# The five-tap convolution of a state-space branch: accumulated in PSUM in three pieces per channel tile instead of in SBUF

## The chip, the cores and the metric

The kernel runs on one core of a Trainium2 chip. Five queues run beside each other on that core: the tensor engine (PE, with its weight loads shown apart as PEld), the vector engine (DVE), the scalar engine (ACT), GpSimd (POOL), and SyncE (SP), which here only issues DMAs. Each takes its instructions strictly in the order in which the program lists them, and waits where an instruction needs something that another engine has not delivered yet. The metric is the device time of one execution in microseconds (us).

## The reference

The program is a two-layer network over 1024 latent tokens and 256 context tokens, 1024 channels wide, in float32. The change lies in layer 0, whose mixer begins with one large input projection. Its results feed, among others, a state-space branch (through a convolution over 5 tokens) and a conformer branch (through a convolution over 31 tokens):

```python
def dwconv(t, w, b):
    pad = w.shape[0] // 2
    y = lax.conv_general_dilated(t, w[:, None, :].astype(t.dtype), window_strides=(1,), padding=[(pad, pad)],
                                 dimension_numbers=('NWC', 'WIO', 'NWC'), feature_group_count=t.shape[-1])
    return y + b

def ssd_branch(z, xbc, dt_raw, h0_f, h0_b, conv_w, conv_b, ...):
    xbc = jax.nn.silu(dwconv(xbc, conv_w, conv_b))        # 5 taps, 1536 channels
...
def conformer_conv(glu_in, w, b, ln_g, ln_b):
    val, gt = jnp.split(glu_in, 2, axis=-1)
    h = dwconv(val * jax.nn.sigmoid(gt), w, b)            # 31 taps, 1024 channels
    return jax.nn.silu(layer_norm(h, ln_g, ln_b))
```

Context (256 tokens) and latents (1024 tokens) are convolved apart, each with its own zero padding.

## The kernel before

The stage in question is `inproj0`. Channels lie on the 128 partitions, tokens along the free dimension. One channel tile is a projection of 128 channels for all 1280 tokens, in three slices of 512, 512 and 256 tokens, one PSUM bank each. Three banks (m0, m1, m2) rotate, so PE can be three slices ahead of the engine that copies a slice out. Each slice is 24 matmuls at L170 (8 parts of the contraction, three products each, for the split of float32 numbers into a high and a low part: `hhi`, `hlo`, `wh`, `wl`). The weights of a tile come by DMA; ACT rounds the high part (`wh`, L157) and DVE subtracts for the low part (`wl`, L158).

The tiles come in this order: GLU tiles 0 to 6 of the conformer branch (a gate and a value projection each), then the twelve tiles of the state-space branch, then GLU tile 7. These twelve are called tiles 1 to 12 here. The first matmul of tile 1 starts at 272.72 us of the profiled execution, and the value projection of GLU tile 7 starts at 510.48 us; this stretch is called the five-tap stage. It holds thirteen projections: tiles 1 to 12 and the gate of GLU tile 7.

For each of the twelve tiles, `xbc` does this:

- POOL zeroes the edges of a buffer `pad` (L1231; two buffers, so tile n waits until the taps of tile n-2 have read theirs).
- ACT copies the three slices out of PSUM to `pad` (L1235).
- ACT multiplies by the first tap into `acc5` in SBUF (L1242), over all 1282 positions.
- DVE does taps 2 to 5, one instruction each over all 1282 positions (L1244): `acc = pad * w + acc`, with `pad` and `acc` both in SBUF.
- ACT applies the silu in two parts (L1245, L1246), and SP stores the two parts (L1247, L1248).

Beside it run the 31-tap convolutions of the GLU tiles, as work to fill in. For GLU tiles 1, 3 and 6 ACT makes the products (L1215, two buffers `prod`) and POOL adds them up (L1216, `accq`, all in SBUF), 30 adds per GLU tile, with a start by ACT (L1212) and a copy back by ACT (L1217, L1218). For the others DVE does 30 steps (L1224): `acc = u * w + acc`, with `u` in SBUF and `acc` in PSUM. In the five-tap stage POOL finishes GLU tile 3 and does GLU tile 6; DVE finishes GLU tile 4 and does GLU tile 5.

The order on every engine is set at build time by a scheduler that estimates durations; the five-tap convolution has high priority and the 31-tap steps a very low one (-3000 and -5000), so they fill what the scheduler believes to be gaps.

## Time and profile before

| what | us |
|---|---|
| median of 3 runs (2262.7 to 2266.95) | 2266.37 |
| the profiled execution, first to last instruction | 2267.6 |
| the five-tap stage in it, 272.72 to 510.48 | 237.8 |
| PE busy in the whole execution | 2148.1 |
| PE idle, waiting for the copy of a slice to `pad` | 35.2 |
| DVE busy in the five-tap stage | 229.3 |

The page of the profile gives busy time by engine, the work that ended last, and the costliest groups of instructions with the idle time before them and what ended it. The trace answers with the waits by pairs of engines, with the instructions of an engine in order of time (start, duration, engine, line, operation, output, inputs, count; in brackets the idle time before, if any), and with the busy time of each engine and the granted clock of PE in any stretch. An instruction's duration overlaps the next one's by up to a tenth of a microsecond, so what a step costs is best read from the distance of two starts.

### The profile page before, as it was taken

What the parts mean: (1) busy time and instruction counts of PE and PEld (TensorE: products, weight loads), DVE (VectorE), ACT (ScalarE), POOL (GpSimd) and SP (SyncE); (2) the same over time, 40 slices, a digit from 0 to 9 for tenths busy, and PEclk for the clock granted to TensorE, in tenths of its full rate; (3) what the DMA queues carried; (4) which work ended last, traced back from release to release, by engine and by line L of the source; (5) the groups of instructions that cost most, each with busy time, mean ns of one, the idle gap of its engine ahead of it and who ended that gap; (6) DMA issues with size and microseconds to landing.
All of it is one profiled execution on the core that took longest, in us unless ns stands there. A gap on an engine that the chain in (4) does not pass through costs nothing.

```text
span 2267.6 us, 28582 instructions
## 1 busy us (share of the span) xinstructions
PE 2148.1 (95%) x10748; PEld 1647.3 (73%) x10748; DVE 1470.1 (65%) x1912; ACT 1005.1 (44%) x1553; POOL 1015.7 (45%) x652
## 2 busy tenths in 40 slices
PE   7998998889999999999999999999999999899997
PEld 6877876769997766656789788888666666666676
DVE  6799999988743377677775133223665566566677
ACT  4355565543552233333333233325556666545510
POOL 0088998870223355444330128433344444424453
PEclk9999999989999999899999999999999999899998
DMA  7121111115535765555434224323112111523363
GB/s 271 57 67 57 42 51 64 63 59 170 180 113 191 249 194 176 169 192 180 140 115 134 75 77 170 128 84 98 51 45 60 31 45 53 161 83 116 111 187 128
DMA packets 160145, 262.79 MB, mean 116 GB/s; under 512 B 19028, under 2 KB 98768, under 8 KB 159752
## 3 DMA queue, kind: packets, MB, share of 16 engines
q1 hardware_dynamic: 158584, 257.45, 34.9%
q0 software_dynamic: 1280, 3.26, 0.5%
q8 instruction: 84, 1.38, 0.2%
q14 instruction: 53, 0.43, 0.1%
q10 hardware_dynamic: 144, 0.26, 0.0%
HBM read 186.55 MB, written 74.32 MB: 115 GB/s over the span
## 4 chain that ended last, share of the span: by engine, by line
PE 58%; DVE 7%; DMA 5%; ACT 3%; issue 2%; POOL 2%; SPq 0%; POOLq 0%; DVEq 0%; ACTq 0%
PE m L170 28%; PE m L1009 12%; PE po L746 4%; PE st L728 2%; PE st L729 1%; PE ms L691 1%; DMA mr<-in_modw_dram 1%; PE m L840 1%; PE po L1542 1%; DVE ml L158 1%; PE ms L686 1%; ACT rb L433 1%; POOL ks L828 1%; PE m L691 1%; PE yd L1563 1%
## 5 line engine op out<-in xcount | busy, mean ns | idle before, releaser
L170 PE MATMUL m<-hhi,wh 128*128 128x512 f32 (+1 forms) x840 | 306.9, 369 | 36.8 <-ACT pad L1235 35.2
L1216 POOL TENSOR_TENSOR accq<-accq,prod 128x1295 f32<-128x1295 f32 x90 | 319.0, 3545 | 43.7 <-ACT prod L1215 30.3
L170 PE MATMUL m<-hlo,wh 128*128 128x512 f32 (+1 forms) x840 | 308.2, 367 | 0.0
L170 PE MATMUL m<-hhi,wl 128*128 128x512 f32 (+1 forms) x840 | 306.1, 365 | 1.0 <-DVE wl L158 1.0
L1224 DVE SCALAR_TENSOR_TENSOR acc<-u,vwh,acc 128x1295 f32<-128x1295 f32 x150 | 234.8, 1565 | 6.1 <-issue 2.2
L739 POOL TENSOR_TENSOR pl<-pt,ph 128x512 fp32r<-128x512 f32 x96 | 129.0, 1344 | 236.7 <-ACT ph L738 227.7
L170 PE MATMUL m<-h1hi,wh 128*128 128x512 f32 (+1 forms) x544 | 218.3, 401 | 2.0 <-ACT rb L433 1.4
L170 PE MATMUL m<-h1lo,wh 128*128 128x512 f32 (+1 forms) x544 | 217.0, 399 | 0.0
L170 PE MATMUL m<-h1hi,wl 128*128 128x512 f32 (+1 forms) x544 | 216.3, 398 | 0.0
L170 PEld LDWEIGHTS m<-hhi,wh 128*128 128x128 f32 x840 | 161.7, 194 | 64.4 <-ACT pad L1235 38.3
L1009 PE MATMUL m<-woh,yh 128*128 128x512 f32 x448 | 187.0, 421 | 0.6 <-ACT yh L157 0.2
L1009 PE MATMUL m<-wol,yh 128*128 128x512 f32 x448 | 185.3, 414 | 1.0 <-DVE wol L158 0.5
L1009 PE MATMUL m<-woh,ylo 128*128 128x512 f32 x448 | 185.0, 413 | 0.5 <-DVE ylo L158 0.5
L170 PEld LDWEIGHTS m<-hhi,wl 128*128 128x128 f32 x840 | 162.6, 194 | 27.9 <-issue 3.4
L170 PEld LDWEIGHTS m<-hlo,wh 128*128 128x128 f32 x840 | 163.0, 194 | 24.6 <-issue 2.4
L1215 ACT ACTIVATE prod<-u,vwh 128x1295 f32<-128x1295 f32 x90 | 123.4, 1378 | 82.0 <-POOL accq L1216 81.9
L738 ACT CAST ph<-pt 128x512 fp32r<-128x512 f32 x152 | 93.1, 619 | 115.3 <-PE po L746 107.9
L158 POOL TENSOR_TENSOR wl<-wr,wh 128x1024 fp32r<-128x1024 f32 x33 | 80.6, 2443 | 122.7 <-ACT wh L157 99.0
L1244 DVE SCALAR_TENSOR_TENSOR acc<-pad,vecs,acc 128x1282 f32<-128x1282 f32 x48 | 131.8, 2748 | 3.2 <-issue 1.8
L170 PEld LDWEIGHTS m<-h1hi,wh 128*128 128x128 f32 x544 | 103.2, 190 | 28.7 <-issue 2.6
L746 PE MATMUL po<-ph,vs 128*66 128x512 f32 x304 | 122.9, 404 | 0.8 <-ACT ph L738 0.8
L731 ACT ACTIVATE pt<-st 128x512 f32<-128x512 f32 x152 | 90.7, 597 | 74.2 <-PE st L729 54.5
(360 smaller groups left out, 4890.2 us busy)
## 6 DMA issues: line engine op xcount, KB each, us to landing
wr<-in_wch_dram SPq DMA_DIRECT2D x69, 512.0 KB
mr<-in_modw_dram SPq DMA_DIRECT2D x64, 256.0 KB
mr<-in_modw_dram SPq DMA_DIRECT2D x16, 512.0 KB
wor<-in_wout_dram SPq DMA_DIRECT2D x16, 512.0 KB
xcT<-xbc_d SPq DMA_DIRECT2D x20, 320.0 KB
xt_d<-xtok SPq DMA_DIRECT2D x20, 320.0 KB
xtok<-xt_d SPq DMA_DIRECT2D x10, 640.0 KB
xt<-xt_d SPq DMA_DIRECT2D x10, 640.0 KB
```

Source lines behind the costliest of these rows:

```text
L158: (nc.gpsimd if pool_lo else nc.vector).tensor_tensor(lo, src, hi.bitcast(F32), op=ALU.subtract)
L170: nc.tensor.matmul(out, x(k), y(k), start=(c == 0), stop=(c == tot - 1))
L691: nc.tensor.matmul(ps[:, :nw], mv1[0:64, b, h], ks1[0:64, C + w0 * P:C + w0 * P + nw], start=True, stop=True)
L731: nc.scalar.activation(p.rearrange("p h t -> p (h t)"), ps, AF.Exp, scale=0.125)
L738: nc.scalar.copy(ph, p)
L739: (nc.gpsimd if x in (0, 1, 3) else nc.vector).tensor_tensor(pl, p, ph.bitcast(F32), op=ALU.subtract)
L746: nc.tensor.matmul(po[:66], vs[:, kb, v], p[y], start=first and i == 0, stop=last and i == 2)
L1009: nc.tensor.matmul(ps[f], y[u][:, k], w[k][v][:, 512 * f:512 * f + 512], start=i + j == 0, stop=i + j == 9)
L1215: nc.scalar.activation(pr, u[:, k:k + N], AF.Copy, scale=vwh[:, i, k:k + 1])
L1216: nc.gpsimd.tensor_tensor(acc, acc, pr, op=ALU.add)
L1224: nc.vector.scalar_tensor_tensor(acc[:, :N], u[:, k:k + N], vwh[:, i, k:k + 1], acc[:, :N], op0=ALU.mult, op1=ALU.add)
L1244: nc.vector.scalar_tensor_tensor(acc, pad[:, k:k + N], w(k), acc, op0=ALU.mult, op1=ALU.add)
```

## The change

`acc` becomes a PSUM tile. The convolution of a channel tile is cut in three pieces of 256, 512 and 512 tokens; each piece takes one of the two buffers of the PSUM bank name `ms`, gets its first tap from ACT, four taps from DVE, and a silu from ACT which writes to an SBUF buffer `out`. One store takes the place of two. The two positions between context and latents that were computed and dropped are no longer computed. The rest of the diff only removes comments.

```diff
             self.proj_ch(wp, W[i], hhi, hlo, ev)
             with tc.high_priority():
-                N = 1282
-                acc = p5.tile([P, 1282], F32, name="acc5", tag="acc5")
                 w = lambda k: self.V("cw", 5 * i + k)
-                nc.scalar.activation(acc, pad[:, 0:N], AF.Copy, scale=w(0))
-                for k in range(1, 5):
-                    nc.vector.scalar_tensor_tensor(acc, pad[:, k:k + N], w(k), acc, op0=ALU.mult, op1=ALU.add)
-                nc.scalar.activation(acc[:, :C], acc[:, :C], AF.Silu, bias=self.V("cb", i))
-                nc.scalar.activation(acc[:, 258:], acc[:, 258:], AF.Silu, bias=self.V("cb", i))
-                nc.sync.dma_start(xbc_d[i, :, :C], acc[:, :C])
-                nc.sync.dma_start(xbc_d[i, :, C:], acc[:, 258:])
+                out = p5.tile([P, T], F32, name="acc5", tag="acc5")
+                for a, n in ((0, 256), (256, 512), (768, 512)):
+                    o = a if a < C else a + 2
+                    acc = self.bank("ms")[:, :n]
+                    nc.scalar.activation(acc, pad[:, o:o + n], AF.Copy, scale=w(0))
+                    for k in range(1, 5):
+                        nc.vector.scalar_tensor_tensor(acc, pad[:, o + k:o + k + n], w(k), acc, op0=ALU.mult, op1=ALU.add)
+                    nc.scalar.activation(out[:, a:a + n], acc, AF.Silu, bias=self.V("cb", i))
+                nc.sync.dma_start(xbc_d[i], out)
```

In the changed kernel the first tap is L1244, the other taps L1246 and the silu L1247. The scheduler orders the stage anew. On POOL, from the adds of GLU tiles 1 and 3 on (the first 54 or 57 adds; each group of three MEMSETs prepares the `pad` of one tile, from tile 3 on):

```order
-L1216 TENSOR_TENSOR accq<-accq,prod 128x1295 x54
+L1216 TENSOR_TENSOR accq<-accq,prod 128x1295 x57
+L1231 MEMSET pad 128x2 x3
+L1216 TENSOR_TENSOR accq<-accq,prod 128x1295 x4
+L1231 MEMSET pad 128x2 x3
+L1216 TENSOR_TENSOR accq<-accq,prod 128x1295 x6
+L1231 MEMSET pad 128x2 x3
+L1216 TENSOR_TENSOR accq<-accq,prod 128x1295 x7
+L1231 MEMSET pad 128x2 x3
+L1216 TENSOR_TENSOR accq<-accq,prod 128x1295 x6
```

The adds now stand some six to a tile; before, three to five stood between two groups of MEMSETs in the same part.

On DVE, the taps of tile 1 (`ms` is the piece in PSUM; `acc` of L1224 is a 31-tap step):

```order
+L1246 SCALAR_TENSOR_TENSOR ms<-pad,vecs,ms 128x256
 L1224 SCALAR_TENSOR_TENSOR acc<-u_792,vwh,acc 128x1295
-L1244 SCALAR_TENSOR_TENSOR acc_2781<-pad,vecs,acc_2781 128x1282
+L1246 SCALAR_TENSOR_TENSOR ms<-pad,vecs,ms 128x512
+L1246 SCALAR_TENSOR_TENSOR ms<-pad,vecs,ms 128x256
 L1224 SCALAR_TENSOR_TENSOR acc<-u_792,vwh,acc 128x1295
-L1244 SCALAR_TENSOR_TENSOR acc_2781<-pad,vecs,acc_2781 128x1282
+L1246 SCALAR_TENSOR_TENSOR ms<-pad,vecs,ms 128x512
```

One tap of 1282 between two 31-tap steps has become one or two shorter taps. In tiles 3 to 5, seven or eight 31-tap steps stand in a tile instead of about four, and from tile 7 on none is left.

On ACT, one tile in the middle of the stage before, from the first copy of tile 6 to the first copy of tile 7 (`m_...` are slices in PSUM):

```order
L1235 COPY pad<-m_3193 128x512
L1215 ACTIVATE prod<-u_794,vwh 128x1295
L1235 COPY pad<-m_3219 128x512
L1215 ACTIVATE prod<-u_794,vwh 128x1295
L157 CAST wh<-wr 128x1024
L1235 COPY pad<-m_3245 128x256
L1242 ACTIVATE acc_3271<-pad,vecs 128x1282
L1215 ACTIVATE prod<-u_794,vwh 128x1295
L1245 ACTIVATE acc_3173<-acc_3173,vecs 128x256
L1246 ACTIVATE acc_3173<-acc_3173,vecs 128x1024
L1235 COPY pad<-m_3291 128x512
```

and in the changed kernel, between the last copy of tile 6 and the first copy of tile 7:

```order
L1215 ACTIVATE prod<-u_794,vwh 128x1295
L1247 ACTIVATE acc_3225<-ms,vecs 128x256
L1215 ACTIVATE prod<-u_794,vwh 128x1295
L1244 ACTIVATE ms<-pad,vecs 128x512
L1215 ACTIVATE prod<-u_794,vwh 128x1295 x2
L1247 ACTIVATE acc_3225<-ms,vecs 128x512
L1244 ACTIVATE ms<-pad,vecs 128x256
L1215 ACTIVATE prod<-u_794,vwh 128x1295
L157 CAST wh<-wr 128x1024
L1215 ACTIVATE prod<-u_794,vwh 128x1295
L1247 ACTIVATE acc_3225<-ms,vecs 128x512
L1235 COPY pad<-m_3369 128x512
```

Three products a tile have become six, and all of them stand ahead of the next tile's first copy. The last product of GLU tile 6 in the changed kernel stands between the first and the second copy of tile 9 (`m_3591`, `m_3617`):

```order
L1215 ACTIVATE prod<-u_794,vwh 128x1295
L1247 ACTIVATE acc_3447<-ms,vecs 128x512
L1215 ACTIVATE prod<-u_794,vwh 128x1295
L1244 ACTIVATE ms<-pad,vecs 128x256
L1247 ACTIVATE acc_3447<-ms,vecs 128x512
L1235 COPY pad<-m_3591 128x512
L1215 ACTIVATE prod<-u_794,vwh 128x1295
L1244 ACTIVATE ms<-pad,vecs 128x512
L1247 ACTIVATE acc_3558<-ms,vecs 128x256
L1235 COPY pad<-m_3617 128x512
```

Before, it stood between the first and the second copy of tile 11. PE's order of work in the stage is the same in both. Behind the stage only a few transposes of the output projection's stage (L1058, around 1150 us) change places with matmuls, and 12 stores fewer are issued by SP.

## Rows read from the trace of the kernel before

**Rows 1.** Costliest groups of the page: busy, mean ns | idle before, releaser.

```profile
L170 PE MATMUL m<-hhi,wh 128*128 128x512 f32 (+1 forms) x840 | 306.9, 369 | 36.8 <-ACT pad L1235 35.2
L1216 POOL TENSOR_TENSOR accq<-accq,prod 128x1295 f32<-128x1295 f32 x90 | 319.0, 3545 | 43.7 <-ACT prod L1215 30.3
...
L1244 DVE SCALAR_TENSOR_TENSOR acc<-pad,vecs,acc 128x1282 f32<-128x1282 f32 x48 | 131.8, 2748 | 3.2 <-issue 1.8
```

**Rows 2.** Busy time by stretch: length, PE, PEld, DVE, ACT, POOL, PE clock, DMA.

```profile
272.70:510.50 237.80, 201.07 (x963) 168.90 (x961) 229.25 (x113) 132.14 (x144) 205.30 (x84) 0.92 0.18 59
```

**Rows 3.** PE in order of time: starts of tile 1, tile 2, last projection.

```profile
272.72 0.40 PE L170 MATMUL m<-hhi,wh 128*128 128x512 f32 x1
...
286.50 0.40 PE L170 MATMUL m<-hhi,wh 128*128 128x512 f32 x1
...
510.48 0.50 PE L170 MATMUL m<-hhi,wh 128*128 128x512 f32 x1 [0.74 <-ACT th L1192]
```

**Rows 4.** Waits in the five-tap stage: total us, times, longest.

```profile
ACT acc L1245 <- DVE acc L1244: 52.4, 10, 14.0
ACT prod L1215 <- POOL accq L1216: 49.0, 32, 2.8
...
PE m L170 <- ACT pad L1235: 35.2, 10, 9.1
```

**Rows 5.** DVE in order of time: 31-tap steps, evacuations and five-tap steps.

```profile
269.86 0.68 DVE L1199 SCALAR_TENSOR_TENSOR u<-th,m 128x512 f32<-128x512 f32 x1
270.46 4.78 DVE L1224 SCALAR_TENSOR_TENSOR acc<-u,vwh,acc 128x1295 f32<-128x1295 f32 x3
...
277.22 0.41 DVE L1199 SCALAR_TENSOR_TENSOR u<-th,m 128x256 f32<-128x256 f32 x1
277.56 1.56 DVE L1224 SCALAR_TENSOR_TENSOR acc<-u,vwh,acc 128x1295 f32<-128x1295 f32 x1
279.03 1.21 DVE L158 TENSOR_TENSOR wl<-wr,wh 128x1024 fp32r<-128x1024 f32 x1
...
343.75 1.55 DVE L1244 SCALAR_TENSOR_TENSOR acc<-pad,vecs,acc 128x1282 f32<-128x1282 f32 x1
...
354.12 2.81 DVE L1244 SCALAR_TENSOR_TENSOR acc<-pad,vecs,acc 128x1282 f32<-128x1282 f32 x1
356.85 1.56 DVE L1224 SCALAR_TENSOR_TENSOR acc<-u,vwh,acc 128x1295 f32<-128x1295 f32 x1
```

**Rows 6.** All 150 instructions of L1224: duration in ns, least, median, most.

```profile
L1224 DVE SCALAR_TENSOR_TENSOR acc<-u,vwh,acc x150: 1551/1567/1574, 97.5 to 574.5; 128x1295 f32<-128x1295 f32 x150
```

**Rows 7.** ACT in order of time: products, and the change from GLU tile 3 to 6.

```profile
279.02 1.39 ACT L1215 ACTIVATE prod<-u,vwh 128x1295 f32<-128x1295 f32 x1 [0.77 <-POOL accq L1216]
...
283.14 1.38 ACT L1215 ACTIVATE prod<-u,vwh 128x1295 f32<-128x1295 f32 x1 [2.26 <-POOL accq L1216]
286.23 1.39 ACT L1215 ACTIVATE prod<-u,vwh 128x1295 f32<-128x1295 f32 x1 [1.71 <-POOL accq L1216]
...
337.80 0.41 ACT L1217 COPY u<-accq 128x256 f32<-128x256 f32 x1 [1.15 <-POOL accq L1216]
...
340.81 1.47 ACT L1212 ACTIVATE accq<-u,vecs,vwh 128x1295 f32<-128x1295 f32 x1
```

**Rows 8.** POOL in order of time: adds of GLU tiles 3 and 6.

```profile
229.89 83.25 POOL L1216 TENSOR_TENSOR accq<-accq,prod 128x1295 f32<-128x1295 f32 x24 [7.76 <-ACT accq L1212]
...
345.48 26.52 POOL L1216 TENSOR_TENSOR accq<-accq,prod 128x1295 f32<-128x1295 f32 x7
...
409.41 2.94 POOL L1216 TENSOR_TENSOR accq<-accq,prod 128x1295 f32<-128x1295 f32 x1
...
462.72 12.15 POOL L1216 TENSOR_TENSOR accq<-accq,prod 128x1295 f32<-128x1295 f32 x3
```

**Rows 9.** Busy time by stretch around one wait of PE (columns as in rows 2).

```profile
460.00:470.00 10.00, 4.84 (x17) 3.77 (x16) 10.00 (x6) 5.33 (x7) 8.51 (x6) 0.68 0.40 118
```

**Rows 10.** DVE in order of time: last weight split ahead of the next stage.

```profile
519.73 0.89 DVE L158 TENSOR_TENSOR zl<-wr,zh 128x704 fp32r<-128x704 f32 x1 [0.84 <-ACT zh L157]
```

## The prediction, made before the changed kernel ran

> **What bounds the kernel now.** I read the page's costliest groups first, then the busy time by stretch, then the waits of the one stretch that stood out, then three engines in order of time in it. PE is busy nearly throughout, and its largest idle time by far is 36.8 us, of which 35.2 us end with ACT's copy of a slice to `pad` [rows 1]. All of it lies in the five-tap stage [rows 4]. There PE needs 286.50 - 272.72 = 13.78 us for a projection when nothing holds it [rows 3]. Thirteen projections are 179.1 us, and the stage takes 510.48 - 272.72 = 237.8 us, so 58.6 us are lost: 237.80 - 201.07 = 36.7 us with PE idle, and 21.9 us with PE busy at less than full clock, 0.92 on the mean [rows 2]. [...]
>
> The copies come late because ACT takes its instructions in order, and stands 52.4 us before silus that wait for DVE's last tap and 49.0 us before products that wait for POOL's adds [rows 4]. So DVE and POOL pace the stage, and they pace each other. A five-tap step beside POOL takes 2.81 us; the same step at 343.75, while POOL waited for its next convolution (337.8 to 345.48), took 1.55 us [rows 5, 7, 8]. POOL's add of the same size takes 286.23 - 283.14 = 3.09 us while DVE does only 31-tap steps [rows 7]. With five-tap and 31-tap steps in turn, one pair takes (356.85 - 354.12) + (279.03 - 277.56) = 4.20 us [rows 5], and the adds keep that pace (12.15 us for three) [rows 8]. The 31-tap step, with its accumulator in PSUM, takes 1551 to 1574 ns in all 150 cases, beside POOL or not [rows 6]. So what makes DVE and POOL stop for each other here is the instruction with two operands in SBUF, and the change turns 48 of these into the harmless form. The subtraction for `wl` stays as it is.
>
> **DVE's taps.** Removed: four steps of 2.73 us a tile, 10.9 us. Added: eight steps of 512 and four of 256. The nearest rows are the evacuations of GLU, one operand in PSUM, at 270.46 - 269.86 = 0.60 and 277.56 - 277.22 = 0.34 us from start to start [rows 5], which gives 8 x 0.60 + 4 x 0.34 = 6.2 us a tile; by their full durations, 0.68 and 0.41, it is 7.1 us. I take 6.5, since in most places a 31-tap step stands between two taps that depend on each other. DVE gets some 4.4 us a tile, 53 us in all, out of 229 busy [rows 2]. That is not the gain, because the scheduler puts 31-tap steps into it.
>
> [...]
>
> **POOL's adds, which lead.** After the change I price an add at 3.09 us, and at 4.12 (283.14 - 279.02) where a `wl` falls in [rows 7]. GLU tile 3 starts at 229.89 as before [rows 8]: 30 x 3.09 + 4 x 1.03 = 96.8, end at 326.7. Then ACT copies back and starts GLU tile 6: from 337.80 to 340.81 + 1.47 it took 4.5 us before [rows 7]; with some 2 us for ACT being at a silu, the adds of GLU tile 6 begin at about 333, not 345.48.
>
> **ACT's order.** In the middle of the stage six or seven products stand between the copies of one tile and of the next, and each waits for POOL, so a tile now takes 6 x 3.09 + 1.03 = 19.6 to 22.7 us there. That is above PE's 13.78, so PE will still wait 4 to 8 us in each of tiles 4 to 8. DVE must keep up: seven or eight steps of 1.47, 6.5 for taps and some 2 us for `wl` (1.21 at 279.03 [rows 5], more where it must wait for one) are 18.8 to 20.3 us, just under POOL's. The copies of tile 8 stand behind the 26th add's product, which waits for the 24th add: 333 + 24 x 3.09 + 5 x 1.03 = 412.3, then the product and two or three short steps of ACT, 415.5. From there four products are left, while PE has five projections to do: tile 9 starts when the first copy of tile 8 frees its bank.
>
> **The tail.** With no 31-tap steps left, a tile in the tail needs 6.5 to 8 us of DVE (more where taps of one piece follow each other directly) and 1.2 to 2 for `wl`, below 13.78. POOL's sums for the conformer stand ahead of the MEMSETs of tiles 11 and 12; at 4 us each, after adds that end near 431, they are done before 460, when tile 12 wants its buffer. So PE runs through: 415.5 + 5 x 13.78 = 484.4. The clock was low for some ten microseconds around a wait [rows 9], which I price at 10 x (1 - 0.68) = 3.2 at most and 2.5 here: 487. The value projection of GLU tile 7 starts 23.5 us earlier than at 510.48.
>
> **What follows it.** PE is then the leader for the next 70 us, so the gain stays only if nothing is late. The 31-tap steps of GLU tile 7 start behind PE's own value projection and move with it. The last weight split of the next stage ended at 520.6, 3 us before that projection did [rows 10]; it hangs on stores of tile 12 that now come about 480, more ahead of PE than before, so this cover grows. One store instead of two frees SP's queue. The few transposes that change places 650 us later cost PE the same. I count all of these at nothing; without that cover, each microsecond by which the split is late would be one of the gain.
>
> **Sum.** 23.5 us off the median of 2266.4 is 2242.9. The profiled execution spans 2267.6, 0.05% over the median, so its durations carry over. The bounds of the likeliest case: with adds at 2.94 us, as the one at 409.41 [rows 8], and no loss of clock, 54 x 0.15 + 2.5 = 10.6 us more gain, 2232; with DVE's `wl` and POOL's adds holding each other for another 1.5 us in five tiles and 3 us more of low clock, 10.5 less, 2253.
>
> **The rivals.**
>
> *Taps in PSUM hold POOL all the same, slower.* The instruction still reads `pad` in SBUF. If an add stayed at 4.20 us, the 35 adds from the first tap of tile 1 to the copies of tile 8 would cost 35 x 1.11 = 39 us more: 415.5 becomes 454, and the stage ends at 526, 15 us late: 2282. It decides from an add of 3.09 + 23.5 / 35 = 3.76 us on. For it: the changed order puts six adds ahead of each copy instead of three. Against it: 31-tap steps read SBUF once too, and the adds beside them take 3.09. 4 in 100.
>
> *Twelve short taps cost DVE more than four long ones.* If POOL were not what stretches a step to 2.81 us, and four long taps cost 1.55 each where it matters, twelve taps at full duration, 7.1 us a tile, would replace four at 1.55, 6.2, and a stage led by DVE would grow by 12 x 0.9 = 11 us: 2277. It decides once short taps take more than the long ones that they replace. Against it stands the step of 1.55 in POOL's pause beside 2.81 with POOL at work. 3 in 100. [...]
>
> *A new lock-step, no change.* If DVE falls behind in tiles 4 to 8, ACT waits at silus, products come late, and POOL waits too. Each of the five tiles would have to take 23.5 / 5 = 4.7 us more than counted, about 25 us. DVE's 20.3 is that near to POOL's pace only if each `wl` loses 4 us. 2266, 7 in 100.
>
> *PE leads from the start.* Then the stage is 179.1 us and the time 2266.4 - 58.6 = 2208. Against it: ACT's order has the products ahead of the copies. 3 in 100; something between this and the forecast is another 3.
>
> **How the numbers follow.** The forecast, 2232 to 2253, has 80 in 100. I widen the range to 2228 to 2260 for half-way cases on both sides. A gain or loss of under 0.2%, 4.5 us, can't be told from no change in this kernel: faster 0.87 (forecast, larger gains, half of what lies between), same 0.06, slower 0.07.
>
> **What would show it.** Right: 512-wide taps of 0.6 to 0.7 us with little spread; adds near 3.09 us in the stage; the last add of GLU tile 6 near 431 instead of 474.9; PE's waits for copies still there in tiles 4 to 8 (20 to 35 us in all) and next to none behind tile 8; the value projection of GLU tile 7 at about 487. Wrong: adds at 4 us, waits of POOL or DVE for ACT in the middle tiles, waits of PE in tiles 9 to 12, or a gain in the stage that is given back before 600 us.

## The result, and the profile after

The changed kernel took 2236.8 us (median of four runs, 2231.1 to 2244.1), the kernel before 2264.5 us beside it; the ratio is 0.988, 95% interval 0.985 to 0.992. The profiled execution after spans 2236.7 us, against 2267.6 before. In a later session the same changed kernel took 2242.8 us, the kernel before 2264.8 beside it, ratio 0.990 (0.987 to 0.993); the two intervals overlap.

Two groups of the page of after answer to [rows 1]; the columns are those of [rows 1].

```profile
L170 PE MATMUL m<-hhi,wh 128*128 128x512 f32 (+1 forms) x840 | 303.7, 365 | 21.0 <-ACT pad L1235 20.2
L1216 POOL TENSOR_TENSOR accq<-accq,prod 128x1295 f32<-128x1295 f32 x90 | 286.8, 3187 | 49.8 <-ACT prod L1215 32.0
```

PE's idle time at this group fell from 36.8 to 21.0 us, and the mean add of POOL from 3545 to 3187 ns. Next the two starts on PE that answer to [rows 3] (tile 1, value projection of GLU tile 7), and the busy time by stretch of what lies between (columns as in [rows 2]).

```profile
274.12 0.40 PE L170 MATMUL m<-hhi,wh 128*128 128x512 f32 x1
...
483.04 0.40 PE L170 MATMUL m<-hhi,wh 128*128 128x512 f32 x1
```

```profile
274.10:483.10 209.00, 188.80 (x939) 160.78 (x938) 186.30 (x209) 138.97 (x179) 169.26 (x84) 0.95 0.19 68
```

For the kernel before, the end of the stage has to be put right first. At 510.48 us, which [rows 3] takes for the start of the value projection of GLU tile 7, that projection's second slice starts, behind a wait for ACT's `th`. Its first slice starts at 503.68, 13 x 72 matmuls behind the start of tile 1 as in the changed kernel:

```profile
503.68 0.63 PE L170 MATMUL m<-hhi,wh 128*128 128x512 f32 x1
```

```profile
272.70:503.70 231.00, 195.02 (x939) 164.28 (x938) 224.72 (x111) 130.04 (x140) 205.30 (x84) 0.92 0.19 60
```

So the stage before is 503.68 - 272.72 = 231.0 us, not 237.8, and 51.8 us of it are lost, not 58.6. After, it takes 483.04 - 274.12 = 208.9 us: 22.0 us less. DVE is busy for 186 us instead of 225, POOL for 169 instead of 205, and PE's clock is 0.95 on the mean instead of 0.92. Ahead of the stage little moved (274.1 us against 272.7). Behind it, 2236.7 - 483.0 = 1753.7 us stand against 2267.6 - 503.7 = 1763.9, but the second execution of the changed kernel has 1760.5. Of the difference to the first, 5.8 us lie in one stretch of attention work over 1100 us behind the stage: 600 matmuls took 164.4 us before, at a granted clock of 0.96 in the mean (0.50 from 1750 to 1760 us), and 158.6 after, at 1.00. With three `pad` tiles the changed kernel took 164.5 us for them too, so this comes and goes and is no gain of the change.

The waits of the stage (total, times, longest) answer to [rows 4]:

```profile
ACT prod L1215 <- POOL accq L1216: 38.7, 30, 2.6
...
PE m L170 <- ACT pad L1235: 20.2, 6, 5.6
ACT acc L1247 <- DVE ms L1246: 11.1, 9, 2.4
```

ACT's wait for DVE's last tap fell from 44.2 us (52.4 in [rows 4], which run to 510.5) to 11.1; its wait for POOL's adds fell less, from 49.0 to 38.7. What is left of PE's waiting has a plain picture on ACT. These are the copies of tiles 6 and 7 of after, in order of time, with some of the products between them:

```profile
377.59 1.34 ACT L1235 COPY pad<-m 128x512 f32<-128x512 f32 x3
...
382.68 1.38 ACT L1215 ACTIVATE prod<-u,vwh 128x1295 f32<-128x1295 f32 x1 [1.33 <-POOL accq L1216]
...
385.77 1.39 ACT L1215 ACTIVATE prod<-u,vwh 128x1295 f32<-128x1295 f32 x1 [1.13 <-POOL accq L1216]
388.85 1.38 ACT L1215 ACTIVATE prod<-u,vwh 128x1295 f32<-128x1295 f32 x1 [1.69 <-POOL accq L1216]
...
396.85 1.34 ACT L1235 COPY pad<-m 128x512 f32<-128x512 f32 x3
```

From tile 4 to tile 7 all three copies of a tile are issued in one go, behind products that wait for POOL, and 396.85 - 377.59 = 19.3 us lie between two such groups, where PE needs 13.78 for a tile. In the stretch from tile 4 to tile 8 POOL is busy for 75.4 of 77.0 us, and DVE for 73.6 (columns as in [rows 2]):

```profile
337.00:414.00 77.00, 62.55 (x288) 52.43 (x288) 73.64 (x78) 55.53 (x68) 75.43 (x37) 0.89 0.18 62
```

### The profile page after: what moved, and what is told of

Same layout as the page of the kernel before. It is cut to its first block, busy times and chain, and to the rows that moved or that the text cites. A ratio compares the mean times of both kernels' runs of the same rounds, so it can differ in the third digit from the quotient of the medians.

```text
span 2236.7 us, 28691 instructions
## 1 busy us (share of the span) xinstructions
PE 2127.9 (95%) x10748; PEld 1636.1 (73%) x10748; DVE 1429.8 (64%) x2008; ACT 1013.3 (45%) x1589; POOL 983.6 (44%) x652
## 4 chain that ended last, share of the span: by engine, by line
PE 48%; DVE 5%; DMA 2%; ACT 2%; POOL 2%; issue 1%; SPq 0%; POOLq 0%; DVEq 0%; ACTq 0%
PE m L170 20%; PE m L1009 11%; PE po L746 4%; PE st L728 2%; PE st L729 1%; PE ms L691 1%; PE m L840 1%; PE po L1542 1%; PE ms L686 1%; ACT rb L433 1%; DMA vs<-rd_d 1%; POOL ks L828 1%; PE m L691 1%; PE ms L481 1%; PE yd L1563 1%
## 5 line engine op out<-in xcount | busy, mean ns | idle before, releaser
L170 PE MATMUL m<-hhi,wh 128*128 128x512 f32 (+1 forms) x840 | 303.7, 365 | 21.0 <-ACT pad L1235 20.2
L1216 POOL TENSOR_TENSOR accq<-accq,prod 128x1295 f32<-128x1295 f32 x90 | 286.8, 3187 | 49.8 <-ACT prod L1215 32.0
L1224 DVE SCALAR_TENSOR_TENSOR acc<-u,vwh,acc 128x1295 f32<-128x1295 f32 x150 | 235.0, 1566 | 8.4 <-ACT acc L1221 3.9
L170 PEld LDWEIGHTS m<-h1hi,wl 128*128 128x128 f32 x544 | 102.4, 188 | 24.5 <-issue 2.0
```

Source lines behind the costliest of these rows:

```text
L170: nc.tensor.matmul(out, x(k), y(k), start=(c == 0), stop=(c == tot - 1))
L1216: nc.gpsimd.tensor_tensor(acc, acc, pr, op=ALU.add)
L1224: nc.vector.scalar_tensor_tensor(acc[:, :N], u[:, k:k + N], vwh[:, i, k:k + 1], acc[:, :N], op0=ALU.mult, op1=ALU.add)
```

## Experiments

The theory to test: a five-tap step with both operands in SBUF and an add of POOL stop for each other; with the accumulator in PSUM they don't, and after the change ACT's products, waiting for POOL, hold the copies. Each comparison gives the stage as the time from PE's first matmul of channel tile 1 to its first of GLU tile 7's value projection. Before it is 231.0 us and after 208.9; the expectations, written with 510.48 as its end, have 237.8.

### Pieces without PSUM

```diff
-                    acc = self.bank("ms")[:, :n]
+                    acc = p5.tile([P, 512], F32, name="accs", tag="accs")[:, :n]
```

> The changed kernel with one thing undone: the accumulator of the three pieces lies in SBUF (two buffers), not in PSUM; pieces, order, silu and the single store are as changed. My theory (what costs before is that a DVE step with two operands in SBUF and a POOL sum stop for each other): the 512-wide steps take 1.0 us or more beside POOL's sums, the sums come back to 3.7 to 3.9 us in the stage against 3.16 after the change, the stage from the first convolution tile's first matmul to GLU 7's value projection goes back to 230 to 242 us, and the kernel takes 2258 to 2272 us. Rival A (the gain is from the cut into pieces and the order that follows, not from PSUM): stage 207 to 214 us, 2234 to 2242 us.

Measured: 2314.1 us, ratio to before 1.021 (1.018 to 1.024). The order on each engine is that of the changed kernel, but for some neighbours that change places. The stage took 281.9 us:

```profile
273.60:555.50 281.90, 197.54 (x939) 166.95 (x938) 270.91 (x209) 139.57 (x179) 172.34 (x84) 0.85 0.14 49
```

Rival A falls: the pieces and their order alone make the kernel 2% slower than before, so the gain hangs on PSUM. My numbers were wrong too, on the small side. The groups of the stage show why (DVE's steps by shape, then POOL's adds; columns as in [rows 1]).

```profile
L1216 POOL TENSOR_TENSOR accq<-accq,prod 128x1295 f32<-128x1295 f32 x48 | 154.9, 3227 | 42.9 <-ACT prod L1215 32.6 <-ACT accq L1212 8.2
L1246 DVE SCALAR_TENSOR_TENSOR accs<-pad,vecs,accs 128x512 f32<-128x512 f32 x96 | 112.1, 1184 | 3.2 <-ACT accs L1244 2.2
...
L1246 DVE SCALAR_TENSOR_TENSOR accs<-pad,vecs,accs 128x256 f32<-128x256 f32 x48 | 65.8, 1371 | 1.6 <-ACT accs L1244 1.1
```

I had expected POOL's adds to pay (3.7 to 3.9 us); they took 3.23. DVE paid: a step of 256 columns took 1371 ns in the mean, more than one of 512. The trace, instruction by instruction, shows why. Of the 144 steps, 101 start while no add of POOL runs, and none of them is held, that is, takes longer than its usual time. The other 43 start during an add, and every one ends just behind that add: 0.28 to 0.29 us behind it with 256 columns, 0.55 us with 512. The first two lines are one such add and step; the third is, in the kernel before, the add that the step at 354.12 of [rows 5] met.

```profile
350.23 3.13 POOL L1216 TENSOR_TENSOR accq<-accq,prod 128x1295 f32<-128x1295 f32 x1 [8.20 <-ACT accq L1212]
350.51 3.13 DVE L1246 SCALAR_TENSOR_TENSOR accs<-pad,vecs,accs 128x256 f32<-128x256 f32 x1
```

```profile
351.62 3.95 POOL L1216 TENSOR_TENSOR accq<-accq,prod 128x1295 f32<-128x1295 f32 x1
```

That add ended at 355.57 and the step at 356.93. So it is throughout the kernel before: 39 of its 48 steps start during an add and end 1.35 to 1.36 us behind it, and the other nine take about 1.55 us. In the changed kernel 110 of the 144 steps, now in PSUM, start during an add, and none is held. So what a step with two operands in SBUF pays here is the rest of the add that it meets, with 256, 512 and 1282 columns alike. The pieces met adds hardly more often than the long steps did (43 times against 39), but earlier in the add, and paid 2.0 us each time against 1.5 (in the mean, over the shortest duration): some 86 us in all against 58. DVE was busy for 270.9 of 281.9 us, as it had been for 224.7 of 231.0 before.

### Half of the tiles in PSUM

```diff
-                    acc = self.bank("ms")[:, :n]
+                    acc = self.bank("ms")[:, :n] if i % 2 else p5.tile([P, 512], F32, name="accs", tag="accs")[:, :n]
```

> The changed kernel with the accumulator in PSUM for the odd channel tiles alone and in SBUF for the even ones. My theory: the steps of the even tiles and the sums beside them are slow, those of the odd tiles fast, so about half of the 28.9 us of the stage is lost: stage 220 to 227 us, 2246 to 2256 us. Rival A (pieces and order make the gain): 2234 to 2242 us. A rival B (the chain is set by few tiles, 4 to 8, three of them even): nearer to before, 2252 to 2260 us.

Here `i` counts tiles from 0, so tiles 2, 4, ..., 12 have PSUM, and of tiles 4 to 8 two lie in SBUF, not three as in rival B.

Measured: 2280.8 us, ratio 1.007 (1.004 to 1.009), stage 247.5 us. None of the three ranges held it: they took before as the worst that SBUF could do, and the first experiment shows 2314 for that. Halfway from 2314.1 to 2236.8 is 2275.5, near what was measured. The kernel has both forms side by side, in one stage, beside the same adds:

```profile
L1246 DVE SCALAR_TENSOR_TENSOR accs<-pad,vecs,accs 128x512 f32<-128x512 f32 x48 | 61.7, 1285 | 1.7 <-ACT accs L1244 1.4
L1246 DVE SCALAR_TENSOR_TENSOR ms<-pad,vecs,ms 128x512 f32<-128x512 f32 x48 | 35.7, 747 | 3.3 <-ACT ms L1244 2.9
L1246 DVE SCALAR_TENSOR_TENSOR accs<-pad,vecs,accs 128x256 f32<-128x256 f32 x24 | 34.0, 1415 | 0.8 <-ACT accs L1244 0.8
...
L1246 DVE SCALAR_TENSOR_TENSOR ms<-pad,vecs,ms 128x256 f32<-128x256 f32 x24 | 11.5, 478 | 0.1
```

The same step of 512 columns takes 1285 ns with its accumulator in SBUF (`accs`) and 747 with it in PSUM (`ms`); of 256 columns, 1415 and 478.

### Before, without POOL's adds

```diff
-                        nc.gpsimd.tensor_tensor(acc, acc, pr, op=ALU.add)
+                        nc.gpsimd.memset(pr[:, :2], 0.0)
```

> The kernel before, with POOL's 90 sums of the 31-tap convolutions of GLU tiles 1, 3 and 6 left out (a fill of two columns in place of each, so that products are still made and released). My theory: without POOL reading SBUF the four 1282-wide steps on two SBUF operands take 1.55 us each instead of 2.81, no step of the stage is above 1.6 us, tensor engine waits fall away, and the stage of 237.8 us falls to 185 to 200 us; what comes behind it falls by as much. Rival C (steps on two SBUF operands are slow by themselves): steps stay at 2.4 us or more and the stage above 220 us.

Measured: 2198.1 us in one run, stage 443.03 - 259.14 = 183.9 us, a little below the expected range. The first line has the five-tap steps in SBUF (least, median and most, in ns), the second the stage.

```profile
L1244 DVE SCALAR_TENSOR_TENSOR acc<-pad,vecs,acc x48: 1542/1551/4236, 279.3 to 437.7; 128x1282 f32<-128x1282 f32 x48
```

```profile
259.10:443.00 183.90, 180.97 (x938) 155.80 (x937) 167.98 (x109) 108.34 (x125) 28.02 (x66) 0.99 0.24 79
```

Rival C falls: the step takes 1.55 us in the median where it took 2.81. Four of the 48 are held; all four start during POOL's sums for the conformer (`csum`), which were left in and read SBUF too. Tile 1 starts 13.6 us earlier, as the GLU tiles ahead of it lost their adds too, and the stage is 47.1 us shorter. The scheduler sets a new order here and in the next two kernels.

### After, without POOL's adds

The same edit in the changed kernel.

> The changed kernel with the same 90 sums left out (a fill of two columns in place of each). It asks what still bounds the stage of 209.0 us after the change. My theory (ACT's products wait for POOL's sums and stand ahead of the copies of tiles 4 to 8): with no sums the stage falls to 180 to 192 us, the tensor engine's waits for the copies are nearly gone. Rival D (DVE with its 50 long and 144 short steps is the bound): the stage stays at 200 us or more, with the waits for the copies ended by DVE.

Measured: 2215.0 us in one run, stage 462.23 - 259.69 = 202.5 us. My theory falls here and rival D's holds. Without any add the changed kernel's stage is only 6.4 us shorter than with all of them, and 18.6 us longer than that of the kernel before without adds. The waits of that stage, then the stretch in which all of PE's waits lie, and DVE's 31-tap steps in it:

```profile
ACT acc L1247 <- DVE ms L1246: 43.6, 16, 7.2
...
DVE wl L158 <- ACT wh L157: 21.1, 6, 4.4
...
PE m L170 <- ACT pad L1235: 16.8, 4, 6.5
```

```profile
300.00:377.00 77.00, 60.18 (x299) 51.04 (x299) 74.21 (x79) 36.73 (x54) 13.92 (x23) 0.92 0.19 65
```

```profile
L1224 DVE SCALAR_TENSOR_TENSOR acc<-u,vwh,acc 128x1295 f32<-128x1295 f32 x28 | 43.8, 1565 | 0.2
```

DVE is busy for only 172.0 of the 202.5 us, but where PE waits, from 300 to 377 us, it is busy for 74.2 of 77.0. The 21.1 us that DVE itself waits for ACT lie mostly behind that, where PE no longer waits. What fills DVE there are 28 steps of the 31-tap convolution, 43.8 us: up to nine of them stand between two weight splits, among the short steps, where the kernel before without adds has two to five. ACT stands at silus that wait for the short steps, and the copies stand behind these. So two kinds of filler hold the copies in the middle of the changed kernel's stage: products, which wait for POOL, and 31-tap steps, which delay the short steps and with them the silus. Taking one away leaves the other. The 18.6 us are a price of the pieces and the order that came with them (one run of each kernel), which the end of the stops for POOL outweighs.

### POOL busy, but reading nothing

```diff
-                        nc.gpsimd.tensor_tensor(acc, acc, pr, op=ALU.add)
+                        nc.gpsimd.memset(pr, 0.0)
+                        nc.gpsimd.memset(pr, 0.0)
+                        nc.gpsimd.memset(pr[:, :640], 0.0)
```

> The kernel before with each of POOL's 90 sums of the 31-tap convolutions replaced by three fills of the product tile (1295, 1295 and 640 columns): POOL stays about as long busy for each product (estimate 2.9 us, from a fill of 1280 columns at 1.17 us in the trace of before) and holds the product buffer as long, but reads nothing from SBUF; the sums of GLU tiles 1, 3 and 6 are left out. My theory (a DVE step with two operands in SBUF stops only for a POOL instruction that reads SBUF): the 1282-wide steps take 1.55 us in the median and the low parts of the weights 1.2 us, as with the sums left out, and the stage takes 185 to 212 us. Rival (POOL being busy, whatever it does, slows the steps, or the stage is set by ACT waiting for product buffers): steps stay at 2.4 us or more, or the stage stays at 230 us or more.

Measured: 2202.6 us in one run, stage 446.82 - 260.24 = 186.6 us. The groups of the stretch from tile 1 to 410 us, ahead of POOL's sums for the conformer (five-tap steps, the three fills, low parts of weights):

```profile
L1246 DVE SCALAR_TENSOR_TENSOR acc<-pad,vecs,acc 128x1282 f32<-128x1282 f32 x40 | 64.6, 1614 | 3.7 <-ACT acc L1244 2.8 <-issue 0.3 <-POOL prod L1216 0.2
...
L1216 POOL MEMSET prod<- 128x1295 f32 x40 | 47.5, 1187 | 15.7 <-ACT prod L1215 15.7
L1217 POOL MEMSET prod<- 128x1295 f32 x39 | 46.3, 1187 | 1.3
L1218 POOL MEMSET prod<- 128x640 f32 x40 | 25.4, 635 | 0.9
...
L158 DVE TENSOR_TENSOR wl<-wr,wh 128x1024 fp32r<-128x1024 f32 x10 | 12.2, 1224 | 3.5 <-ACT wh L157 3.5
```

POOL is busy for 1.19 + 1.19 + 0.64 = 3.0 us for each product, as with an add, and DVE does not notice: 1.61 us for a five-tap step in SBUF and 1.22 for a `wl`, the value of [rows 5]. Of the 48 five-tap steps 31 start during a fill, and none is held. So it is not that POOL is busy, nor that products wait for POOL; what is left is that an add reads SBUF and a fill doesn't. (No run had POOL read one operand only.) When POOL's sums for the conformer, which read SBUF, began at 408.04, the five-tap steps grew at once; the five that are held all start during one of these sums:

```profile
407.95 5.72 DVE L1246 SCALAR_TENSOR_TENSOR acc<-pad,vecs,acc 128x1282 f32<-128x1282 f32 x2
...
417.50 8.40 DVE L1246 SCALAR_TENSOR_TENSOR acc<-pad,vecs,acc 128x1282 f32<-128x1282 f32 x2
```

In the mean a five-tap step of 1282 columns took 2.75 us in the kernel with adds [rows 1], and 1.61 in the one with fills, up to 410 us.

### Another pad tile

In the changed kernel the three copies of tiles 4 to 7 come in one go. My guess was that they wait in the order for a free `pad` tile, of which there are two, and that a third one lets the order put copies between products.

```diff
-            pad = p5.tile([P, 1286], F32, name="pad", tag="pad")
+            pad = p5.tile([P, 1286], F32, name="pad", tag="pad", bufs=3)
```

In the kernel before:

> The kernel before with three pad tiles in place of two, and nothing else: in ACT's order the copies of a tile no longer stand three in a row behind 6 to 8 products, but between them. My theory: the slow steps keep DVE busy for about 229 us of the stage whatever the order, so the stage stays at 228 to 240 us and the kernel at 2256 to 2270 us. Rival (ACT's order is what costs in the kernel before, and the change gains by another order): stage under 220 us, under 2248 us.

Measured: 2267.4 us, ratio 1.000 (0.999 to 1.002), stage 233.2 us, and steps of 2.81 us in the median. This says little about ACT's order, because the expectation starts from something that isn't so: in the kernel before, the copies of nearly every tile stand between products already, and the third `pad` tile moved two copies forward, the first ones of tiles 6 and 8, and nothing on DVE. What it shows is that DVE is busy for 98% of the stage:

```profile
273.10:506.40 233.30, 192.15 (x939) 161.16 (x938) 229.15 (x112) 129.99 (x140) 206.15 (x81) 0.93 0.19 59
```

What speaks against the rival is the kernel with its pieces in SBUF, which has the changed kernel's order and gains nothing by it.

In the changed kernel:

> The changed kernel with three pad tiles in place of two, and nothing else. My theory (after the change the tensor engine waits for copies that stand on ACT behind 6 to 7 products of a tile, each waiting for a POOL sum of 3.16 us): with the copies between the products the waits of 20.2 us mostly go, the stage of 209.0 us becomes 188 to 200 us, the kernel takes 2216 to 2230 us. Rival (POOL's 48 sums or DVE's 186 us of work bound the stage whatever ACT's order): within 3 us of the changed kernel, 2233 to 2240 us.

Measured: 2232.1 us, ratio to before 0.986 (0.983 to 0.988), stage 472.81 - 271.48 = 201.3 us. It falls between the two ranges: 7.6 us less in the stage, and a total that can't be told from that of the changed kernel. PE still waited 17.1 us for copies (20.2 after the change), since tiles 7 to 9 had their three copies in one go, behind products:

```profile
375.17 1.34 ACT L1235 COPY pad<-m 128x512 f32<-128x512 f32 x3
...
394.32 1.33 ACT L1235 COPY pad<-m 128x512 f32<-128x512 f32 x3
...
414.38 1.35 ACT L1235 COPY pad<-m 128x512 f32<-128x512 f32 x3
```

### Pacing the fillers

Order can also be forced. With three pad tiles, the products of GLU tile 6 and the 31-tap steps of GLU tile 5 are emitted in `xbc`, a few for each channel tile, each behind an instruction of that tile on its own engine. The core of the edit (`mark` holds the tile's copies, `taps` its five-tap steps; `later` the two convolutions as generators of steps; PP = 4, TP = 3, TD = 2, where `i` counts tiles from 0). The first products and the copies back of the 31-tap convolutions get the low priority of the steps, too:

```diff
+        def some(key, ins, n, prio):
+            with tc.high_priority(prio), tc.issue_after(ins.ins):
+                for _ in range(n):
+                    next(later[key], None)
...
+            if i >= TP:
+                for j, m in enumerate(mark):
+                    some("p", m, PP * (j + 1) // 3 - PP * j // 3, -3000)
+            if PD and i >= TD:
+                for j in range(PD):
+                    some("d", taps[12 * j // PD], 1, -5000)
```

With PD = 3, three 31-tap steps a tile:

> The changed kernel with three pad tiles, and with the steps of two GLU tiles paced by the channel tile: from tile 3 on, four products and sums of GLU 6 for each tile, each put behind one of that tile's copies on ACT; from tile 2 on, three 31-tap steps of GLU 5 for each tile, each put behind one of that tile's short steps on DVE; what is left of GLU 5 comes behind the stage. My theory: sums take 4 x 3.16 = 12.6 us a tile and DVE 7.5 + 3 x 1.48 + 2.1 = 14.0 us against the tensor engine's 13.8, so the stage comes to 172 to 184 us, and the kernel to 2200 to 2212 us, as long as what is pushed behind the stage is hidden there. Rival (it is not hidden: GLU 7's convolution and the layer norm behind it become late): 2212 to 2236 us.

Measured: 2230.1 us, ratio 0.985 (0.982 to 0.987). The stage came to 453.69 - 273.50 = 180.2 us as expected, and PE was busy throughout it, but the total lies in the rival's range. The stage is not all that was before it: 23 of the 144 short steps come behind its end, the last at 477.7 us. The first line is the stage, the next two the 50 us from 457 on, and the last the wait in them.

```profile
273.50:453.70 180.20, 179.46 (x939) 154.61 (x938) 165.37 (x181) 128.68 (x164) 163.42 (x79) 1.00 0.21 70
```

```profile
457.00:482.00 25.00, 11.88 (x62) 9.89 (x60) 24.28 (x30) 10.02 (x16) 5.12 (x2) 0.81 0.20 70
482.00:507.00 25.00, 23.59 (x144) 23.32 (x145) 22.81 (x18) 7.15 (x20) 0.67 (x1) 0.91 0.60 195
```

```profile
479.46 1.25 PE L170 MATMUL m<-zh,hhi 128*128 128x352 f32 x3 [11.83 <-ACT zh L157]
```

The stage's gain over the changed kernel, 28.7 us, was partly given back at once, though not by what the rival names: PE waited 11.8 us for the first z weight, whose rounding stood on ACT behind silus and a copy that waited for late DVE steps, and worked at a granted clock of 0.81 and 0.91 around it.

With PD = 1, and the other 20 steps behind the last tile's:

> As the paced kernel, but one 31-tap step of GLU 5 for each channel tile instead of three, so that 20 of its 30 steps come after the last tile's short steps. In the paced kernel the tensor engine lost 11.8 us behind the stage, because DVE ran late, ACT stood in its order ahead of the next weights' rounding, and the clock fell. My theory: DVE has 7.5 + 1.5 + 2.1 = 11.1 us a tile against the tensor engine's 13.8, is on time at the end of the stage, and the 11.8 us go; the 20 steps (30 us) are hidden beside the z projections. Stage 170 to 182 us, 2202 to 2216 us. Rival (the 20 steps make GLU 7's convolution and the layer norm late, and that is not hidden): 2222 us or more.

Measured: 2225.8 us, ratio 0.983 (0.980 to 0.985), stage 179.9 us. With PD = 2 and TD = 4:

> As the paced kernel, but two 31-tap steps of GLU 5 for each channel tile, from tile 4 on: 16 of 30 within the stage. My theory: DVE 7.5 + 3.0 + 2.1 = 12.6 us a tile against 13.8, on time as with one step, 2202 to 2216 us, within 4 us of the kernel with one step. Rival (DVE is late again at the end, since its short steps wait for each other): the wait behind the stage stays at 5 us or more, 2216 to 2232 us.

Measured: 2229.1 us, ratio 0.985 (0.982 to 0.987), stage 179.5 us. Both totals lie in the rivals' ranges. Of the 11.8 us the first has 2.3 left; the second has none at that place, but 3.7 us for a later z weight, at 572. New waits came: 3.0 us for evacuations on DVE in the first, 3.1 us for channel tiles that are loaded back to be transposed in the second. In both, long steps still stood between the last short ones and ahead of the evacuations. These waits are only 5.3 and 6.8 us, while the part behind the stage takes 1771 and 1773 us, against 1754 and 1761 in the two executions of the changed kernel; where the rest went is not shown here. The changed kernel ran beside these two:

> The changed kernel itself once more, beside the paced ones on the same chip: 2233 to 2240 us by every theory.

Measured: 2242.8 us, 2.8 us above the range, with a stage of 483.48 - 274.52 = 209.0 us as before. So these two beat it by 17 and 14 us.

Last, with PD = 2 and TD = 4, the 14 steps that are left behind DVE's last evacuation of GLU tile 7 (`last` holds it):

```diff
-                if PD:
-                    with tc.high_priority(-5000):
-                        run(later["d"])
...
+                if i == 7 and PD:
+                    some("d", last[0], 32, -5000)
```

> As the kernel with two 31-tap steps of GLU 5 for each channel tile from tile 4 on, but the 14 that are left are put behind DVE's last evacuation of GLU 7's value projection, so that the short steps of the last tile and the low parts of the first z weights stand ahead of them. In the two kernels before it some 10 us of the stage's gain were given back between the stage and the first gates, where the tensor engine waited for roundings and evacuations and its clock fell. My theory: these waits came from DVE's long steps between the last short ones; now they go, the stage stays at 178 to 184 us and the kernel takes 2208 to 2220 us. Rival (the long steps have only moved, and hold the later z weights or the layer norm): 2222 to 2232 us.

Measured: 2214.0 us, ratio to before 0.978 (0.975 to 0.980), as the theory said. The stage, then the 50 us behind it:

```profile
273.20:452.80 179.60, 179.34 (x938) 154.52 (x937) 162.65 (x188) 133.35 (x172) 163.91 (x79) 1.00 0.22 77
```

```profile
453.00:478.00 25.00, 24.05 (x134) 21.32 (x134) 16.98 (x20) 7.83 (x16) 0.00 (x0) 1.00 0.42 130
478.00:503.00 25.00, 25.00 (x166) 24.90 (x165) 21.47 (x14) 8.98 (x25) 5.90 (x2) 1.00 0.45 146
```

The stage lasts 452.83 - 273.17 = 179.7 us. That is thirteen projections at 13.78, 179.1 us, so PE bounds it, at a clock of 1.00, and PE runs on through the next 50 us. All 48 adds are in it, so POOL's adds did not need 208.9 us. DVE's share fell from 186.3 to 162.7 us, mostly since steps of GLU tile 5 moved out (6 of the 144 short steps come behind the stage, too). By these figures I estimate that with all of them the stage could not be much shorter than 186 us. What lies between that and 208.9 I put down to order; the one run that changed order alone, with three `pad` tiles, came to 201.3.

## Why the prediction was right, step by step

- **The mechanism** held: what costs here is the instruction with two operands in SBUF beside a POOL add, which reads SBUF. The half-and-half kernel shows the first part (1285 ns against 747 for 512 columns), the fills the second (1.61 us against 2.75 for 1282). That also settles the rival of taps that hold POOL from PSUM: adds in the stage took 3.16 us in the mean. One reading for it was wrong without harm: POOL's pause before 345.48 was not a wait for its next convolution, whose start on ACT was done at 342.28 [rows 7], but for DVE's taps, which a clear of `pad` at 345.36 waited for.
- **The end of the stage before** was misread. The value projection of GLU tile 7 started at 503.68, and not at 510.48, so my own working, which puts it at 487 after the change, gives a gain of 16.7 us and 2249.7, not 23.5 and 2242.9. It started at 483.04, 20.6 us earlier than before, and PE went on to the z projections 22.1 us earlier (496.82 against 518.93), since before it was slower at the start of that projection (0.63 us for the matmul at 503.68, 0.40 at 483.04). So 6.8 us too much at one end stood against 4.0 too little at the other; that 23.5 lies between the measured gains of 27.7 and 22.0 us (2264.5 to 2236.8, and 2264.8 to 2242.8 in the later session) is in part luck. The last split of [rows 10] did not end 3 us before that projection, which ended at 519, but 1.5 us behind it; PE did not wait for it.
- **DVE's taps** were sized a little low. By full durations I had 7.1 us a tile as the bound; it was 8 x 0.750 + 4 x 0.483 = 7.9. One step took 476, 746 and 759 ns (least, median and most over both widths) where the evacuation of GLU took 0.41 and 0.68 [rows 5], and the sign of 0.6 to 0.7 us for 512 columns, with little spread, held for the spread alone. From start to start I took 6.5 us; where a 31-tap step follows, a step of 256 and one of 512 columns together take 362.51 - 361.46 = 1.05, and one of 512 alone 0.66, which makes 6.8. It did no harm to the forecast, because POOL and ACT's order led.

```profile
L1246 DVE SCALAR_TENSOR_TENSOR ms<-pad,vecs,ms x144: 476/746/759, 294.7 to 479.1; 128x512 f32<-128x512 f32 x96, 128x256 f32<-128x256 f32 x48
```

```profile
361.46 1.14 DVE L1246 SCALAR_TENSOR_TENSOR ms<-pad,vecs,ms 128x256 f32<-128x256 f32 x2
362.51 1.56 DVE L1224 SCALAR_TENSOR_TENSOR acc<-u,vwh,acc 128x1295 f32<-128x1295 f32 x1
```

- **POOL's adds** came as worked out. The adds of GLU tile 3 ended at 330.1 (326.7 predicted, with a start 1.4 us later), those of GLU tile 6 began at 334.26 (333) and ended at 430.8 (431), against 474.9 before [rows 8]. The runs of adds between the clears of `pad` show it:

```profile
334.26 2.94 POOL L1216 TENSOR_TENSOR accq<-accq,prod 128x1295 f32<-128x1295 f32 x1 [4.17 <-ACT accq L1212]
...
356.54 23.05 POOL L1216 TENSOR_TENSOR accq<-accq,prod 128x1295 f32<-128x1295 f32 x7
...
424.72 6.11 POOL L1216 TENSOR_TENSOR accq<-accq,prod 128x1295 f32<-128x1295 f32 x2
```

- **ACT's order** was right for tiles 4 to 8: copies at 337.28, 356.28, 377.59, 396.85 and 413.41, steps of 19.0, 21.3, 19.3 and 16.6 us where I had 19.6 to 22.7, so three of four a little shorter; PE waited 20.2 us, at the foot of 20 to 35. POOL led there and DVE stood just under it, as worked out (75.4 and 73.6 of 77.0 us). What I didn't see is how little POOL alone is worth: without any add the stage lost only 6.4 us, because DVE with its 31-tap steps takes over.
- **The tail** was bound by PE, as predicted. The copies of tile 8 came at 413.41 instead of 415.5, and 413.41 + 5 x 13.78 = 482.3, where 483.04 was measured. The 2.5 us for a low clock were not lost: from 410 us on the granted clock was 1.00. These two terms, 2.1 and 2.5 us, less the 0.7 us, are the 4.0 us between 487 and 483.04.
- **Nothing was given back** behind the stage: 1753.7 and 1760.5 us in two executions, against 1763.9.
- **The rival of twelve short taps** had 3 in 100 and is refuted as an outcome, but there is something in it: without adds the changed kernel's stage is 202.5 us, and that of the kernel before 183.9. DVE's work explains 4 of the 18.6 us (172.0 us busy against 168.0). That the rest is order, with more 31-tap steps among the short ones of a tile, is read from DVE's busy time where PE waits, and fits the last paced kernel, which has two of them a tile; but no run changed their places alone. In the changed kernel this price is hidden in a gain that I estimate at 44 us (231.0 to 186.6, from the kernel with fills) if the stops went without the pieces.
- **The rival in which PE leads from the start** priced the kernel at 2208, and with the 51.8 us that were really lost it would be 2214.6. The change doesn't reach it; the last paced kernel does, at 2214.0, with a stage of 179.7 where that rival had 179.1.

## What to carry to other kernels

Look for DVE steps with both operands in SBUF that start during a POOL add in SBUF. In the kernel before and in the one with its pieces in SBUF all 82 of them ended behind that add, 0.28 to 0.29 us with 256 columns, 0.55 with 512 and 1.35 to 1.36 with 1282. With the accumulator in PSUM none of 110 was held, and beside fills, which only write, none of 31. So try these two, an operand in PSUM or POOL work that only writes, before cutting such steps into smaller ones: the pieces and their order alone made the kernel 2% slower. Once such stops are gone, look at what stands in order ahead of the copies that free PE's banks: two kinds of filler may hold them, and taking away one shows little. Judge the bound where the waits are: DVE's share of the whole stage hid that it was full there. Fillers can be paced by the tile and put behind the tile's own instructions, but what is pushed out of a stage must also stand behind the first things that the next stage needs.

## What the hardware showed beyond that

- The stop works both ways, so who pays changes with the mix. In the kernel before, 38 of the 47 adds of L1216 that start in the stage start during a DVE instruction with two operands in SBUF (a tap or a `wl`). Each of them ends 2.78 to 2.88 us behind that instruction, and they take 4.04 us in the mean; the other nine take 2.94 to 3.02. With twelve short steps a tile in SBUF 37 adds start so, but a short step is soon over, and the adds took 3.23 us in the mean, close to 3.16 after the change.
- A step with its accumulator in PSUM is hardly slower than one in SBUF that meets nothing: the shortest of 256 columns took 476 ns after the change and 468 in the kernel with pieces in SBUF.

```profile
L1246 DVE SCALAR_TENSOR_TENSOR accs<-pad,vecs,accs x144: 468/746/3490, 294.3 to 554.3; 128x512 f32<-128x512 f32 x96, 128x256 f32<-128x256 f32 x48
```

- The stops that the change leaves are still there: `wl`, with two operands in SBUF, takes 2.00 us in the mean of its 13 in the stage of after, and 1.22 beside fills. That is some 10 us of DVE's time; no run here moved one of its operands to PSUM.
